# Block transposes on VectorE for K and the outputs in the second pass of a hybrid decoder layer

## The chip, the cores and the metric

The kernel runs on one core of a Trainium2 chip. The core has five engines with a queue each: TensorE (PE, matrix products and its own transposes), VectorE (DVE), ScalarE (ACT), GpSimd (POOL), and SyncE (SP, which here issues most of the DMAs). Each works through its own list of instructions in order and waits at semaphores for the others. The metric is the device time of one execution in microseconds (us), lower is better. The kernel before takes 1733.4 us, the median of three runs that lie between 1732.51 and 1734.95 us.

## The reference, cut to what matters

One layer over 2048 tokens of width 1024: a normed input `h`, one large input projection, a pooling branch A, a gated linear recurrence B (HGRN2, eight heads of 128), a gated merge, an output projection and a residual. The change touches branch B only:

```python
f = lb + (1.0 - lb) * jax.nn.sigmoid(zf)          # forget gate
logf = jnp.log(jnp.maximum(f, 1e-30))
k = 1.0 - f
q = jax.nn.silu(hq.astype(jnp.float32)).reshape(shp)
v = hi.astype(jnp.float32).reshape(shp)
o = hgrn2(q, k, v, logf)                          # S_t = diag(f_t) S_{t-1} + k_t v_t^T, o_t = S_t^T q_t
o = rms_norm(o, hgrn_norm_g[l]).astype(x.dtype).reshape(b, s, HGRN_WIDTH)
branch_b = (o * jax.nn.silu(hg)) @ w_hgrn_o[l]
```

In chunks, the recurrence needs three things of K: the scores of K against Q inside a chunk (channels must lie on the partitions), the update of the state `k * decay to the end of the chunk` against V (tokens must lie on the partitions), and, for the output, the scores against V plus Q against the state. The output comes out with tokens on the partitions, is normed there, and is needed with channels on the partitions for the next projection. So K and the output each have to be transposed once.

## The kernel before, in words

The tokens are worked in two passes of 1024 (p = 0, 1), each in two halves t = 0, 1 of T = 512 columns, that is four chunks of 128. All data is fp32; large products are formed from a high and a low part (three matmuls per weight tile, `three`, L355), and a Strassen-like scheme (`quad`, L625) makes the two column halves of two projections from seven products B11, T1, T2, B21, T3, B22, T4 of twelve matmuls each. Several products add into one PSUM bank one after another, and in between the bank is read. So T4 adds into bank `a` behind T3, and VectorE must first have read that bank for the sum at L651 (`c22fq<-pafq,c22fq` in the `fq` quad).

For each head h, three quads follow one another: `fq` (forget gate and query), `m` (the merge gates) and `gp` (pooling value or gate, and the output gate); in the last head `gp` comes before `m`. After each product but the first, and once after each quad, `htick` steps every active generator to its next `yield`. That is 21 ticks for each head.

`hgrn` (L677) is such a generator, one for each head and half. Its ticks, counted from the end of the head's `fq`:

- ticks 1 to 3 make F, K, the products TT of the decays and the first operands.
- tick 5, 9 and 14 run `scores` (32 small matmuls of K against X on PE into the bank `psa`), copy the masked results to PT on VectorE (`put`, L720) and multiply K and Q by decays (`kup` and `qup`, L710 to L716).
- tick 19 runs the last sixteen small score matmuls; then `kup(32)` and `kup(64)` (L812, L813) bring K to the end of the chunk.
- tick 21: four PE transposes bring K into the PSUM tile `pk` (L819), and ScalarE copies it to SBUF as `KS` (L821).
- tick 23: `pd` = KS against V (L826), and a chain of four VectorE instructions to carry the state `SC` (L831).
- tick 26: `po`, the output (L839, L840), its sums of squares on ScalarE, and the norm's factor on GpSimd.
- tick 28: ScalarE scales `po` to `on` in SBUF (L854).
- tick 30: four PE transposes bring `on` into the PSUM tile `pot` (L859), VectorE multiplies by the norm's weight and the gate (L861), and SP stores the result (`Gd`, L1026).

Ticks 22 and later fall into the next head, whose own generators run beside them: tick 30 of one head is tick 9 of the next. A pair of generators (t = 0, 1) is stepped in each tick, so transposes come in groups of eight. `pv_got` (L866, even heads) and `pg_got` (L889, odd heads) put the pooling branch's VectorE work into the `gp` quad, that is into ticks 9 to 15; the chain of `W` additions in `pv_got` has one step in head 0, two in head 2, three in head 4 and four in head 6.

The order on PE in the second pass is fixed by hand: with `line["on"]` every matmul and transpose is tied behind the one before it (L345 to L353). The order on the other engines is set by a scheduler that goes by a cost model and the order of the program: an instruction is moved ahead where it is ready and the engine would be idle. SBUF tiles come from one pool of NU = 76 slots (`utile`), PSUM tiles `pk`, `pd`, `po` and `pot` from a pool of two (`px`). Weights for the quads are loaded by SP four tiles ahead (LOOK = 4).

Of the kernel before, what the change touches and what calls it, by code (L numbers as in the profile page):

```python
# [8 lines left out]
F32 = mybir.dt.float32  # L9
# [9 lines left out]
P = 128  # L19
SEQ = 2048  # L20
D = 1024
T = 512
NT = T // P
# [3 lines left out]
NH = 8  # L27
# [8 lines left out]
GAP = 5  # L36
# [36 lines left out]
def tile_block(ctx: ExitStack, tc: tile.TileContext, x, w_ada, b_ada, g_post, w_in, pool_w, w_pool_o, w_hgrn_o,  # L73
               w_out, ident_d, mask_d, icnt_d, w_pv_t, x_t, w_quad, w_po, rows_d, out):
    nc = tc.nc
    V, A, G, PE, SP = nc.vector, nc.scalar, nc.gpsimd, nc.tensor, nc.sync
# [14 lines left out]
    px = ctx.enter_context(tc.tile_pool(name="px", bufs=2, space=bass.MemoryType.PSUM))  # L91

    def utile(name, dt=F32):
        return up.tile([P, T], dt, tag="u", name=name)
# [4 lines left out]
    def after(ins):  # L99
        return tc.issue_after(ins.ins) if ins is not None else nullcontext()  # L100
# [245 lines left out]
    def mm(o, l, r, start, stop):  # L346
        with after(line["it"] if line["on"] else None):
            line["it"] = PE.matmul(o, lhsT=l, rhs=r, start=start, stop=stop, skip_group_check=True)  # L348
        return line["it"]

    def turn(o, i):
        with after(line["it"] if line["on"] else None):
            line["it"] = PE.transpose(o, i, ident)  # L353

    def three(ps, w, rhs, start, stop):  # L355

        hi, lo = w
        n = len(rhs)
        for k in range(n):
            wh, wl = hi[:, k * P:(k + 1) * P], lo[:, k * P:(k + 1) * P]  # L360
            rh, rl = rhs[k]
            mm(ps, wh, rh, start and k == 0, False)
            mm(ps, wh, rl, False, False)
            mm(ps, wl, rh, False, stop and k == n - 1)
# [126 lines left out]
    def v2(ap, n):  # L491
        return ap.rearrange("p (a b) -> p a b", b=n)

    def bc(ap, n):
        return ap.unsqueeze(2).broadcast_to([P, ap.shape[1], n])

    def tt(o, a, b, op=MUL, e=None):
        return (e or V).tensor_tensor(o, a, b, op=op)  # L498
# [126 lines left out]
    def quad(name, cx, got, tick):  # L625
# [3 lines left out]
        def prod(ps, nm, start):  # L629
            three(ps, take(), [mv[nm, i] for i in range(4)], start, True)  # L630
# [45 lines left out]

    def hgrn(p, h, t, cx):  # L677
        n = f"{p}_{h}_{t}"
        F, Q = cx["F"].pop((h, t)), cx["Q"].pop((h, t))
        A.activation(F, F, AF.Identity, bias=lb[:, h:h + 1], scale=oml[:, h:h + 1])  # L680
        V.tensor_scalar(F, F, 1e-30, None, op0=MAX)  # L681
# [2 lines left out]
        K = utile("K" + n)  # L684
# [5 lines left out]
        o = 0  # L690
        for hh in (1, 2, 4, 8, 16, 32, 64):
            w = T // (2 * hh)
            a = v2(Tb[hh], 2)
# [10 lines left out]
        def te(hh, i):  # L704
            return v2(Tb[hh], 2)[:, :, i]

        def vv(cc):
            return vh[:, t * NT + cc, :]

        def kup(hh):  # L710
            a = v2(K, 2 * hh)[:, :, 0:hh]
            tt(a, a, bc(te(hh, 1), hh))

        def qup(hh):
            a = v2(Q, 2 * hh)[:, :, hh:2 * hh]
            tt(a, a, bc(te(hh, 0), hh))  # L716
# [3 lines left out]
        def put(dst, src):  # L720

            w = src.shape[2]
            if len(dst.shape) == 3:
                m = mask[:, moff[0]:moff[0] + 4 * w].rearrange("p (a b) -> p a b", b=w)
                moff[0] += 4 * w
                shp = [P, NT, 4, w]
                V.copy_predicated(dst.rearrange("p (c a) b -> p c a b", c=NT), m.unsqueeze(1).broadcast_to(shp),  # L727
                                  src.unsqueeze(2).broadcast_to(shp))
                return
            a, b = dst.shape[2:]  # L730
            m = mask[:, moff[0]:moff[0] + NB * w].rearrange("p (c q a b) -> p c q a b", c=NT, q=4, b=b)
            moff[0] += NB * w
            V.copy_predicated(dst.rearrange("p (c q) a b -> p c q a b", c=NT), m,  # L733
                              src.rearrange("p c (a b) -> p c a b", b=b).unsqueeze(2)
                              .broadcast_to([P, NT, 4, a, b]))

        def blk(ap, b, hh):

            r = ap.rearrange("p (b a w) -> p b a w", b=b, w=2 * hh)[:, :, :, hh:2 * hh]
            return r[:, :, 0, :] if T // b == 2 * hh else r  # L740
# [12 lines left out]
        def scores(X):  # L753
            for i in range(NB):
                r0 = (i % 4) * 32
                mm(s48[r0:r0 + 32, i // 4, 0:48], K[:, i * 32:(i + 1) * 32], X[:, i, :], True, True)
# [25 lines left out]
        for hh in (2, 8):  # L782
            scores(X)
            put(blk(ptf, NB, hh), s48[:, :, 0:16])
            put(blk(ptf, NB, 2 * hh), s48[:, :, 16:32])
            put(blk(ptf, NB, 2 * hh), s48[:, :, 32:48])
            kup(hh)
            kup(2 * hh)
            if hh == 2:
                X = build(8, NB, 16)  # L790
            else:
                X = qp.tile([P, T], F32, tag="qr", name=f"X32_{n}")
                x32 = X[:, 0:T // 2].rearrange("p (b w) -> p b w", w=32)
                A.copy(x32, blk(Q, NB // 2, 32))
                qup(32)
                x64 = X[:, T // 2:T].rearrange("p (b w) -> p b w", w=64)
                tq = Tb[32].rearrange("p (a b) -> p a b", b=4)
                q64 = blk(Q, NT, 64)
                tt(x64, q64, bc(tq[:, :, 1], 64))
            for _ in range(GAP):  # L800
                yield
        s64 = s48
        for cc in range(NT):
            o = cc * P
# [4 lines left out]
        A.copy(pt[0:64, :, 64:128], s64[0:64, :, 32:96])  # L809
        A.copy(pt[0:32, :, 32:64], s64[0:32, :, 0:32])  # L810
        A.copy(pt[64:96, :, 96:128], s64[64:96, :, 0:32])
        kup(32)  # L812
        kup(64)  # L813
        tt(q64, x64, bc(tq[:, :, 0], 64))
        yield
        yield
        pk = px.tile([P, T], F32, tag="px", name="pk" + n)
        for cc in range(NT):
            turn(pk[:, cc * P:(cc + 1) * P], K[:, cc * P:(cc + 1) * P])  # L819
        KS = utile("KS" + n)  # L820
        A.copy(KS, pk)  # L821
        yield
        yield
        pd = px.tile([P, NT, P], F32, tag="px", name="pd" + n)
        for cc in range(NT):
            mm(pd[:, cc, :], KS[:, cc * P:(cc + 1) * P], vv(cc), True, True)  # L826
        SC = utile("SC" + n)
# [3 lines left out]
            V.scalar_tensor_tensor(nxt, sts[-1], Tb[128][:, cc:cc + 1], pd[:, cc, :], op0=MUL, op1=ADD)  # L831
            sts.append(nxt)
        carry[h] = sts[NT]
        yield
        yield
        yield
        po = px.tile([P, NT, P], F32, tag="px", name="po" + n)
        for cc in range(NT):
            mm(po[:, cc, :], pt[:, cc, :], vv(cc), True, False)  # L839
# [12 lines left out]
        on = utile("on" + n)  # L852
        for cc in range(NT):
            A.activation(on[:, cc * P:(cc + 1) * P], po[:, cc, :], AF.Copy, scale=ss[:, cc:cc + 1])  # L854
        yield
        yield
        pot = px.tile([P, T], F32, tag="px", name="pot" + n)
        for cc in range(NT):
            turn(pot[:, cc * P:(cc + 1) * P], on[:, cc * P:(cc + 1) * P])  # L859
        og = cx["G"].pop((h, t))  # L860
        V.scalar_tensor_tensor(og, pot, col("ng"), og, op0=MUL, op1=MUL)  # L861
        two_out("G", p, h, t, og, cx, h == NH - 1)
# [507 lines left out]
    for p in range(NPASS):  # L1370
# [3 lines left out]
        if p == 0:  # L1374
# [14 lines left out]
            late = [lambda k=k: h_in(0, 1, k, cxs[0]) for k in range(KT)]  # L1389
# [48 lines left out]
        for h in range(NH):  # L1438
            if 0 < h < NH - 1:
                v_head(p, h + 1, cx)  # L1440
            n = f"{p}_{h}"
# [80 lines left out]
        late = []  # L1522
# [75 lines left out]
```

## Time and profile before

| | |
|---|---|
| median of three runs | 1733.4 us |
| the profiled execution, its own time | 1732.42 us |
| span in its profile | 1730.6 us |
| PE busy | 1706.8 us (99%) |
| VectorE busy | 1223.3 us (71%) |
| ScalarE busy | 853.2 us (49%) |
| granted TensorE clock | 1.0 |
| transposes on PE (`pk` and `pot`, both passes) | 256 |

The page of the profile gives busy time of each engine, the chain of waits that ended last, and groups of instructions. A view by stretches of time gives the busy time of every engine in each stretch; the timeline lists single instructions with start, duration, engine, line, and what they write and read ("sq" is Q, "c22fq" and "c12fq" are results of the quad that become Q and F). `x8` means eight instructions merged in one row, and the duration is then from the first start to the last end. Matmuls are pipelined, so the duration of one is longer than the distance from its start to the next one's. The heads of the second pass run from about 981 to 1535 us of the span, 69.2 us each.

### The profile page before, as it was taken

Reading aid. Unit: us, or ns where it says so; the run is one execution under the profiler, and the core shown is the slowest. Engines: PE = TensorE matmul, PEld = TensorE weight load, DVE = VectorE, ACT = ScalarE, POOL = GpSimd, SP = SyncE. Lnnn points to the kernel's source line nnn. Section 1 sums busy time; section 2 is a strip of 40 time slices with the busy share of each in tenths; the row PEclk is TensorE's granted clock in tenths of the full one; section 3 lists DMA queues with packets and bytes.
Section 4 is the critical chain, followed back from the end, with each engine's and each line's share of the span. In section 5 each row is a group of like instructions: output and inputs, shape, how many; then the busy total and the mean of one; then the engine's idle time right before and its main releaser. Section 6 shows DMA issues by size and latency. Waiting matters only on the chain.

```text
span 1730.6 us, 31715 instructions
## 1 busy us (share of the span) xinstructions
PE 1706.8 (99%) x11805; PEld 1405.1 (81%) x11805; DVE 1223.3 (71%) x2546; ACT 853.2 (49%) x1951; POOL 96.5 (6%) x151
## 2 busy tenths in 40 slices
PE   7999999999999999999999999999999999999998
PEld 4788888888888887878888888888888888888886
DVE  4668888897988889788787254455455545776666
ACT  5746656566565665342755334344343343434243
POOL 1100000000000000100030000000000000000002
PEclk9999999999999999999999999999999999999999
DMA  9759888788789788976795765665655655565657
GB/s 331 259 185 323 287 303 287 286 300 314 268 293 329 262 289 286 350 252 223 267 313 179 249 208 179 205 202 176 214 193 173 220 180 194 184 226 168 212 197 265
DMA packets 191262, 425.33 MB, mean 246 GB/s; under 512 B 19282, under 2 KB 44546, under 8 KB 191108
## 3 DMA queue, kind: packets, MB, share of 16 engines
q1 hardware_dynamic: 181748, 406.46, 69.2%
q10 hardware_dynamic: 9360, 16.85, 2.6%
q8 instruction: 93, 1.52, 0.4%
q14 instruction: 61, 0.50, 0.1%
HBM read 267.51 MB, written 155.71 MB: 245 GB/s over the span
## 4 chain that ended last, share of the span: by engine, by line
PE 91%; DVE 4%; DMA 2%; ACT 2%; issue 1%; SPq 0%; POOL 0%; DVEq 0%; ACTq 0%; POOLq 0%
PE pafq L348 10%; PE pagp L348 10%; PE pam L348 9%; PE psA L348 5%; PE pegp L348 5%; PE pefq L348 5%; PE pem L348 5%; PE psV L348 4%; PE raB L348 4%; PE psa L348 4%; PE ray L348 3%; PE pbfq L348 3%; PE po L348 2%; PE pbgp L348 2%; PE pbm L348 2%; PE raV L348 2%
## 5 line engine op out<-in xcount | busy, mean ns | idle before, releaser
L193 DVE TENSOR_TENSOR whl<-wr,whl 128x512 fp32r<-128x512 f32 x160 | 109.4, 689 | 38.1 <-ACT whl L192 31.2
L192 ACT CAST whl<-wr 128x512 fp32r<-128x512 f32 x160 | 99.5, 625 | 69.6 <-issue 18.0
L348 PE MATMUL pam<-hT,whl 128*128 128x512 f32 x384 | 128.2, 394 | 0.6 <-ACT c12m L634 0.5
L348 PE MATMUL pagp<-hT,whl 128*128 128x512 f32 x384 | 128.1, 394 | 0.4 <-ACT c12gp L634 0.4
L348 PE MATMUL pafq<-hT,whl 128*128 128x512 f32 x384 | 126.3, 390 | 0.0
L192 ACT CAST whl<-wri 128x512 fp32r<-128x512 f32 x76 | 47.1, 622 | 118.4 <-PE psA L348 31.5
L733 DVE COPY_PREDICATED PT<-mask,psa 128x256 f32<-128x256 uint8 x160 | 86.1, 547 | 11.9 <-PE psa L348 11.9
L348 PEld LDWEIGHTS pagp<-hT,whl 128*128 128x128 f32 x384 | 72.1, 188 | 16.3 <-ACT c12gp L634 0.5
L348 PEld LDWEIGHTS pam<-hT,whl 128*128 128x128 f32 x384 | 72.1, 188 | 15.8 <-ACT c12m L634 1.1
L348 PEld LDWEIGHTS pafq<-hT,whl 128*128 128x128 f32 x384 | 72.1, 188 | 15.2 <-ACT c12fq L634 0.2
L348 PE MATMUL psA<-Ph,whl 128*128 128x512 f32 x256 | 82.5, 395 | 0.6 <-ACT Ph L179 0.6
L348 PE MATMUL psV<-whl,hB 128*128 128x512 f32 x256 | 79.6, 394 | 1.2 <-ACT hB L1330 1.1
L498 DVE TENSOR_TENSOR K<-K,TT 128x256 f32<-128x256 f32 x192 | 80.4, 423 | 0.0
L348 PE MATMUL pagp<-lT,whl 128*128 128x512 f32 x192 | 74.9, 390 | 0.0
L348 PE MATMUL pam<-lT,whl 128*128 128x512 f32 x192 | 74.8, 390 | 0.0
L348 PE MATMUL pafq<-lT,whl 128*128 128x512 f32 x192 | 74.7, 389 | 0.0
L193 DVE TENSOR_TENSOR whl<-wri,whl 128x512 fp32r<-128x512 f32 x76 | 51.8, 686 | 23.8 <-ACT whl L192 23.0
L727 DVE COPY_PREDICATED PT<-mask,psa 128x256 f32<-128x256 uint8 (+1 forms) x96 | 52.0, 542 | 21.7 <-PE psa L348 21.7
L348 PEld LDWEIGHTS psa<-X,K 128*32 128x32 f32 x2816 | 48.6, 110 | 19.8 <-issue 17.5
L861 DVE SCALAR_TENSOR_TENSOR sgg<-pot,vec,sgg 128x512 f32<-128x512 f32 x32 | 23.1, 746 | 54.5 <-PE pot L353 54.5
L681 DVE TENSOR_SCALAR F<-F 128x512 f32<-128x512 f32 x16 | 6.8, 426 | 77.5 <-ACT F L680 77.4
L348 PEld LDWEIGHTS psV<-whl,hB 128*128 128x128 f32 x256 | 47.5, 188 | 14.0 <-ACT hB L1330 1.4
(568 smaller groups left out, 4786.7 us busy)
## 6 DMA issues: line engine op xcount, KB each, us to landing
wr<-in_w_quad_dram SPq DMA_DIRECT2D x88, 256.0 KB, 4.1
whl<-scr_y SPq DMA_DIRECT2D x36, 512.0 KB, 4.7
sm<-Sd SPq DMA_DIRECT2D x64, 256.0 KB, 5.3
whl<-scr_b SPq DMA_DIRECT2D x32, 512.0 KB, 4.0
scr_y<-rfy SPq DMA_DIRECT2D x40, 256.0 KB, 2.9
x<-in_x_dram SPq DMA_DIRECT2D x32, 256.0 KB, 4.8
wa<-in_w_ada_dram SPq DMA_DIRECT2D x32, 256.0 KB, 6.0
V<-Vd SPq DMA_DIRECT2D x16, 512.0 KB, 5.1
```

The lines of the kernel that those rows point to most:

```text
L192: A.copy(w[:, 0:T], raw)
L193: V.tensor_tensor(w[:, T:2 * T], raw, w[:, 0:T].bitcast(F32), op=SUB)
L348: line["it"] = PE.matmul(o, lhsT=l, rhs=r, start=start, stop=stop, skip_group_check=True)
L498: return (e or V).tensor_tensor(o, a, b, op=op)
L681: V.tensor_scalar(F, F, 1e-30, None, op0=MAX)
L727: V.copy_predicated(dst.rearrange("p (c a) b -> p c a b", c=NT), m.unsqueeze(1).broadcast_to(shp), src.unsqueeze(2).broadcast_to(shp))
L733: V.copy_predicated(dst.rearrange("p (c q) a b -> p c q a b", c=NT), m, src.rearrange("p c (a b) -> p c a b", b=b).unsqueeze(2) .broadcast ...
L861: V.scalar_tensor_tensor(og, pot, col("ng"), og, op0=MUL, op1=MUL)
```

## The change: block transposes on VectorE

In the second pass, heads 0 to 6 (`by_dve`), both transposes go from PE to VectorE. `V.transpose` turns 32x32 blocks; one instruction here takes 32 partitions and four chunks (32x128 elements) and writes them to another set of 32 partitions. Sixteen of them make one transpose of 128x512. `block_turn` issues four, for one group of 32 output partitions.

For K the scaled copy is made at tick 14, right behind the third scores, into a new tile KD (three VectorE multiplications in the place of the two `kup`s at tick 19), so that K itself stays as it is for the last scores. The turns into KS follow in ticks 15 to 18. `pk` and ScalarE's copy are gone. `pd` and the state's chain move from tick 23 to tick 21 in even heads (`late` = 2) and to tick 19 in odd heads; `po` stays at tick 26. The output is turned into an SBUF tile `ot` in ticks 31 to 34 (10 to 13 of the next head), and the multiplication at L861 and the store move from tick 30 to tick 34. In the first pass and in head 7 all stays as before.

```diff
+    def block_turn(dst, src, j):
+        d, s_ = (a.rearrange("p (c n) -> p c n", n=P) for a in (dst, src))
+        for i in range(4):
+            V.transpose(d[32 * j:32 * j + 32, :, 32 * i:32 * i + 32], s_[32 * i:32 * i + 32, :, 32 * j:32 * j + 32])
...
     def hgrn(p, h, t, cx):
         n = f"{p}_{h}_{t}"
+        by_dve, late = p > 0 and h < NH - 1, 2 * (h % 2 == 0)
...
                 tt(x64, q64, bc(tq[:, :, 1], 64))
-            for _ in range(GAP):
+                if by_dve:
+                    KD, KS = utile("KD" + n), utile("KS" + n)
+                    tt(v2(KD, 64)[:, :, 0:32], v2(K, 64)[:, :, 0:32], bc(te(32, 1), 32))
+                    for o in (0, 32):
+                        tt(v2(KD, P)[:, :, o:o + 32], v2((KD, K)[o // 32], P)[:, :, o:o + 32], bc(te(64, 1), 32))
+            for j in range(GAP):
+                if by_dve and hh == 8 and j:
+                    block_turn(KS, K if j == 4 else KD, j - 1)
                 yield
...
-        kup(32)
-        kup(64)
+        if not by_dve:
+            kup(32)
+            kup(64)
         tt(q64, x64, bc(tq[:, :, 0], 64))
-        yield
-        yield
-        pk = px.tile([P, T], F32, tag="px", name="pk" + n)
-        for cc in range(NT):
-            turn(pk[:, cc * P:(cc + 1) * P], K[:, cc * P:(cc + 1) * P])
-        KS = utile("KS" + n)
-        A.copy(KS, pk)
-        yield
-        yield
+        if by_dve:
+            for _ in range(late):
+                yield
+        else:
...
-        yield
-        yield
-        yield
+        for _ in range(7 - late if by_dve else 3):
+            yield
         po = px.tile([P, NT, P], F32, tag="px", name="po" + n)
...
-        yield
-        yield
-        pot = px.tile([P, T], F32, tag="px", name="pot" + n)
-        for cc in range(NT):
-            turn(pot[:, cc * P:(cc + 1) * P], on[:, cc * P:(cc + 1) * P])
+        if by_dve:
+            pot = utile("ot" + n)
+            yield
+            yield
+            for j in range(4):
+                yield
+                block_turn(pot, on, j)
+        else:
...
         og = cx["G"].pop((h, t))
         V.scalar_tensor_tensor(og, pot, col("ng"), og, op0=MUL, op1=MUL)
```

More of the change, by code (lines that the diff above doesn't have):

```diff
@@ L811, in hgrn @@
         A.copy(pt[64:96, :, 96:128], s64[64:96, :, 0:32])
-        kup(32)
-        kup(64)
+        if not by_dve:
+            kup(32)
+            kup(64)
         tt(q64, x64, bc(tq[:, :, 0], 64))
-        yield
-        yield
-        pk = px.tile([P, T], F32, tag="px", name="pk" + n)
-        for cc in range(NT):
-            turn(pk[:, cc * P:(cc + 1) * P], K[:, cc * P:(cc + 1) * P])
-        KS = utile("KS" + n)
-        A.copy(KS, pk)
-        yield
-        yield
+        if by_dve:
[4 more added lines that the diff above has]
+            yield
+            pk = px.tile([P, T], F32, tag="px", name="pk" + n)
+            for cc in range(NT):
+                turn(pk[:, cc * P:(cc + 1) * P], K[:, cc * P:(cc + 1) * P])
+            KS = utile("KS" + n)
+            A.copy(KS, pk)
+            yield
+            yield
         pd = px.tile([P, NT, P], F32, tag="px", name="pd" + n)
@@ L833, in hgrn @@
         carry[h] = sts[NT]
-        yield
-        yield
-        yield
+        for _ in range(7 - late if by_dve else 3):
+            yield
         po = px.tile([P, NT, P], F32, tag="px", name="po" + n)
@@ L854, in hgrn @@
             A.activation(on[:, cc * P:(cc + 1) * P], po[:, cc, :], AF.Copy, scale=ss[:, cc:cc + 1])
-        yield
-        yield
-        pot = px.tile([P, T], F32, tag="px", name="pot" + n)
-        for cc in range(NT):
-            turn(pot[:, cc * P:(cc + 1) * P], on[:, cc * P:(cc + 1) * P])
+        if by_dve:
+            pot = utile("ot" + n)
+            yield
+            yield
+            for j in range(4):
+                yield
+                block_turn(pot, on, j)
+        else:
+            yield
+            yield
+            pot = px.tile([P, T], F32, tag="px", name="pot" + n)
+            for cc in range(NT):
+                turn(pot[:, cc * P:(cc + 1) * P], on[:, cc * P:(cc + 1) * P])
         og = cx["G"].pop((h, t))
```

## The prediction

> **What bounds the kernel now.** I read the page, then the view by stretches for single heads of the second pass, then the timelines of PE and VectorE there.
>
> ```profile
> span 1730.6 us, 31715 instructions
> PE 1706.8 (99%) x11805; PEld 1405.1 (81%) x11805; DVE 1223.3 (71%) x2546; ACT 853.2 (49%) x1951; POOL 96.5 (6%) x151
> PE 91%; DVE 4%; DMA 2%; ACT 2%; issue 1%; SPq 0%; POOL 0%; DVEq 0%; ACTq 0%; POOLq 0%
> ...
> 1257.80:1327.00 69.20, 69.20 (x574) 57.96 (x573) 39.03 (x96) 28.54 (x75) 2.40 (x4) 1.00 0.59 191
> 1327.00:1396.20 69.20, 69.20 (x574) 57.95 (x573) 36.55 (x92) 27.76 (x71) 2.40 (x4) 1.00 0.62 198
> ```
>
> The last two rows are an even head (4) and an odd one (5): the stretch, its length, then busy PE, weight loads, VectorE, ScalarE, GpSimd, the clock, the DMA share. PE is never idle, at a granted clock of 1.00. VectorE works 36.55 to 39.03 of 69.2 us. So PE work taken out here is time won, as long as no new wait of PE on VectorE appears.
>
> **What PE gives up.** How long a matmul is listed says nothing of its price, since they overlap; I go by starts. First `pot` with the scores behind it and a place where the same scores follow a product directly; then `pk`, and a plain change of product.
>
> ```profile
> 1292.76 0.40 PE L348 MATMUL pegp<-hT,whl 128*128 128x512 f32 x1
> 1293.00 1.03 PE L353 MATMUL pot<-ident,on 128*128 128x128 f32 x8
> 1293.96 0.89 PE L348 MATMUL psa<-X,K 128*32 128x48 f32 x64
> ...
> 1308.31 0.39 PE L348 MATMUL pagp<-hT,whl 128*128 128x512 f32 x1
> 1308.63 0.89 PE L348 MATMUL psa<-X,K 128*32 128x48 f32 x64
> ...
> 1327.41 0.39 PE L348 MATMUL pefq<-hB,whl 128*128 128x512 f32 x1
> 1327.64 0.39 PE L348 MATMUL pafq<-hT,whl 128*128 128x512 f32 x1
> 1327.86 0.39 PE L348 MATMUL pafq<-lT,whl 128*128 128x512 f32 x1
> ...
> 1399.32 0.39 PE L348 MATMUL pafq<-hT,whl 128*128 128x512 f32 x1
> 1399.55 1.03 PE L353 MATMUL pk<-ident,K 128*128 128x128 f32 x8
> 1400.34 0.48 PE L348 MATMUL pam<-hB,whl 128*128 128x512 f32 x1
> 1400.66 0.40 PE L348 MATMUL pam<-lB,whl 128*128 128x512 f32 x1
> ```
>
> Eight `pot` transposes cost (1293.96 - 1292.76) - (1308.63 - 1308.31) = 0.88 us; eight `pk` cost (1400.66 - 1399.32) - (1327.86 - 1327.41) = 0.89 us. A head has one group of each. Seven heads: 7 x 1.77 = **12.4 us** off PE. That is the most the change can bring; the listed 272 ns each would say 30 us, and would be wrong. ScalarE's copy of `pk` goes too, 14 x 0.59 us, but ScalarE works 28 of 69 us in these heads and nothing waits on this copy except `pd`: I count it as nothing. `pd`, `po` and the scores keep their number.
>
> ```profile
> L821 ACT COPY KS<-pk 128x512 f32<-128x512 f32 x16 | 8.6, 593 | 0.0
> ```
>
> **What VectorE takes on.** A pair of generators issues 2 x 16 turns for K and 2 x 16 for the outputs: 64 a head, 448 in all, each 128 elements long on 32 partitions. No VectorE transpose is in the trace. The nearest rows are instructions of 128 elements:
>
> ```profile
> L831 DVE SCALAR_TENSOR_TENSOR SC<-SC,TT,pd 128x128 f32<-128x128 f32 x56 | 19.4, 346 | 1.7
> L498 DVE TENSOR_TENSOR TT<-TT 128x128 f32<-128x128 f32 x16 | 4.5, 284 | 0.0
> ...
> 1340.28 0.28 DVE L498 TENSOR_TENSOR TT<-TT 128x128 f32<-128x128 f32 x1
> 1340.48 0.34 DVE L831 SCALAR_TENSOR_TENSOR SC<-SC,TT,pd 128x128 f32<-128x128 f32 x1
> ```
>
> The lower end is 0.20 us, the distance from that TENSOR_TENSOR's start to the next start: neighbours overlap by 0.08 us. The upper end is 0.346 us, the dearest instruction of this length, with no overlap. I take the whole 0.284 us of the SBUF-to-SBUF row, without overlap, since each turn reads and writes other partitions than the one before it, which no instruction in these rows does. The Trainium skill bears on this choice and speaks against the change. Its page "VectorE: DVE Perf Modes", section "Two Vector instructions with no wait between them", says that an instruction whose input or output starts in another group of 32 partitions than the last one's is held until every earlier one has finished; the overlap rows above are all of instructions that start at partition 0, so no run here shows it. By that rule 0.284 is right and 0.20 is not.
>
> Call the price c. 64c is 18 us a head, and VectorE has 30 free on the mean. The mean doesn't decide: it must be done **by two dates**. The turns of outputs can begin when `on` is there (four of each half); the K turns end before `pd` in odd heads (tick 19), and in even heads before `c22fq` (L651), which stands behind them in program order and must read its bank before T4.
>
> ```profile
> 1288.24 0.36 ACT L854 ACTIVATE on<-po,ss 128x128 f32<-128x128 f32 x1
> 1288.75 1.92 ACT L854 ACTIVATE on<-po,ss 128x128 f32<-128x128 f32 x7
> ...
> 1323.38 0.69 DVE L498 TENSOR_TENSOR c22fq<-pafq,c22fq 128x512 f32<-128x512 f32 x1 [0.81 <-PE pafq L348]
> 1324.10 0.42 DVE L498 TENSOR_TENSOR sq<-X,TT 128x256 f32<-128x256 f32 x1
> 1324.77 0.69 DVE L498 TENSOR_TENSOR sq<-c22fq,sq 128x512 f32<-128x512 f32 x1
> ...
> 1326.05 0.42 DVE L498 TENSOR_TENSOR sq<-X,TT 128x256 f32<-128x256 f32 x1
> 1326.38 0.42 DVE L498 TENSOR_TENSOR K<-K,TT 128x256 f32<-128x256 f32 x1
> ...
> 1392.56 0.69 DVE L498 TENSOR_TENSOR c22fq<-pafq,c22fq 128x512 f32<-128x512 f32 x1 [0.75 <-PE pafq L348]
> 1393.28 0.43 DVE L498 TENSOR_TENSOR sq<-X,TT 128x256 f32<-128x256 f32 x1
> ...
> 1405.91 1.95 PE L348 MATMUL pd<-V,KS 128*128 128x128 f32 x16
> ...
> 1151.40:1189.20 37.80, 37.80 (x347) 31.02 (x347) 20.58 (x45) 11.45 (x28) 0.00 (x0) 1.00 0.60 198
> 1289.70:1327.60 37.90, 37.90 (x348) 31.11 (x347) 21.80 (x47) 11.61 (x28) 0.00 (x0) 1.00 0.62 199
> 1428.10:1465.90 37.80, 37.80 (x348) 31.01 (x347) 23.00 (x49) 11.51 (x28) 0.00 (x0) 1.00 0.60 197
> ...
> 1082.20:1117.20 35.00, 35.00 (x335) 28.69 (x334) 16.71 (x36) 9.26 (x19) 0.00 (x0) 1.00 0.66 215
> ...
> 1359.00:1394.00 35.00, 35.00 (x336) 28.70 (x334) 16.77 (x37) 9.26 (x19) 0.00 (x0) 1.00 0.68 217
> ```
>
> The first three stretches, heads 2, 4 and 6, run from the first half's `on` (the fourth of eight ends near 1289.7) to the start of T4 (1327.64). Head 4: VectorE is busy 21.80 us, of which 2.7 lie behind `c22fq` (1324.10 to 1326.80), so 19.1 us are due before it. KD adds per half one multiplication of 256 elements (0.33 us from start to start, 1326.05 to 1326.38) and two of 128 (0.20): 1.5 us for both. The two `kup`s that go, 4 x 0.33 us, lay behind `c22fq` and free nothing in time. The stretch loses `pot`'s 0.9 us. Room: 37.9 - 0.9 - 19.1 - 1.5 = 16.4 us for 64 turns, c up to 0.256. Likewise head 2: 37.8 - 0.9 - 17.9 - 1.5 = 17.5, c up to 0.274; head 6 (one more `W` in each half) 15.1, c up to 0.236. In the odd heads 1, 3 and 5 (the first and the last of three like stretches are shown) the date is `pd`, at 1394.0. Busy 16.7, less the 1.4 from `c22fq` on (1392.56), which isn't due before `pd`: 15.3. The second half's `pd` needs its KS about 0.85 us later than the first's (half of the 1.7 us over which the sixteen matmuls start). Room: 35.0 - 0.9 + 0.85 - 15.3 - 1.5 = 18.15, c up to 0.284. Head 0 has no outputs of a head before it in its stretch, so only half of the turns: no stall.
>
> At c = 0.284 PE is held up 64 x (0.010 + 0.028 + 0.048) = **5.5 us** in heads 2, 4 and 6, and nothing in the odd ones. Net 12.4 - 5.5 = 6.9 us. The profiled execution took 1732.42 us (its span plus 1.8), 1.0 below the median; from the median 1733.4 - 6.9 = **1727 us**.
>
> The ledger assumes that idle slots of VectorE are filled with turns that are ready; the trace shows the scheduler doing so (at 1324.10 tick 19's L814 runs ahead of the query's own multiplication of 1324.77, which is earlier in the program). The multiplication L861 only moves. The later output store stands on SP's queue ahead of weight loads; a load leaves about 9 us before its use and lands in 4.7:
>
> ```profile
> 1308.73 0.32 SPq L203 DMA_DIRECT2D whl<-scr_('fq', 5)_3_5551  x1
> 1317.74 0.39 PE L348 MATMUL pbfq<-hB,whl 128*128 128x512 f32 x1
> whl<-scr_y SPq DMA_DIRECT2D x36, 512.0 KB, 4.7
> ```
>
> So a store that is up to 4.3 us late costs nothing. `gp` is read back only after head 7. KS, KD and `ot` take SBUF slots in place of slots that `TT` and KS free earlier, because `pd` comes earlier; I count nothing.
>
> **The rivals.** (1) Turns overlap as other VectorE instructions do, c = 0.20 to 0.25: stalls are at most 0.9 us, in head 6, and PE keeps all 12.4 us: **1721 us**. For it: every pair of short instructions in the timeline overlaps. Against: none of them changes partitions.
>
> (2) The turn is dearer, and VectorE becomes the bound between `on` and T4 or `pd`. Past 0.284 the stalls sum to 64 x (6c - 1.617) us (1.617 is the sum of the six rooms); they eat the 12.4 us at c = 0.302, and from there on the kernel is **slower**. At the upper row, 0.346, they are 29.4 us: 1733.4 + 17.0 = **1750 us**. For it: the even heads are short of room already at 0.256. Against: transposes have one input and no PSUM operand, as the 346 ns row has.
>
> (3) c lies close to 0.30 and gain and stalls cancel: **1733 us**. The Trainium skill's same page, section "The three transpose paths", gives 311 ns for a VectorE transpose of 128x128 in bf16. By that figure and the hold, an estimate from the page, the sum would be 15.9 us of stalls and 1737 us.
>
> (4) A store of outputs waits on SP by more than the 4.3 us, because VectorE runs later than the scheduler assumed; the weight loads behind it come late. Three us past the slack in six heads would be 18 us against 12.4: **1739 us**. Against: the store's queue is free of this before.
>
> (5) The change doesn't act, because PE's transposes are hidden: excluded by the starts above, save 1 in 50.
>
> **How the numbers follow.** A measurement of this kernel can tell about 0.2%, 3.5 us, from no change; that is c from 0.293 to 0.311. Forecast (c from 0.25 to 0.293) 0.31; rival 1 0.21; rival 3 with 5 0.18; rival 2 0.25; rival 4 0.05. Faster 0.31 + 0.21 = 0.52, same 0.18, slower 0.30. The likeliest one's own range is 1721 to 1730. For 8 in 10 it must reach rival 1 (1721, less 2 for spread) and most of rival 2, to c = 0.34, where the stalls are 27.1 us: 1748.
>
> **What would show it.** PE's `pk` and `pot` groups fall from 128 to 72 each; the groups of VectorE show 448 turns at L358, and the distance between their starts is c. If I am right, PE idles a few us in heads 4 and 6 ahead of T4 (`pafq` waits for `c22fq`), less in 2, hardly in odd heads ahead of `pd`. No such wait: rival 1. Waits in all six: rival 2. Waits of PE on `whl`: rival 4. I am wrong if turns are cheap and PE still waits, or if `c22fq` is put ahead of the turns and `pd` alone is late.

## The result and the profile after

The changed kernel takes **1778.6 us** (median of four runs, 1778.2 to 1780.7) against 1733.6 of the kernel before on the same chip: a ratio of 1.0265, 95% interval 1.0253 to 1.0277. It is slower by 45 us, where 6.4 us faster was forecast. The profiled execution took 1780.71 us, with a span of 1778.9 us.

Rows of the page of the changed kernel: span, busy time of the engines, the chain that ended last by engine, and the three groups of turns (L358 is the transpose in `block_turn`).

```profile
span 1778.9 us, 31939 instructions
PE 1711.8 (96%) x11693; PEld 1401.5 (79%) x11693; DVE 1356.7 (76%) x3008; ACT 845.5 (48%) x1937; POOL 97.3 (5%) x151
...
PE 77%; DVE 16%; DMA 3%; issue 2%; ACT 1%; SPq 0%; POOL 0%; DVEq 0%; ACTq 0%; POOLq 0%
...
L358 DVE STREAM_TRANSPOSE ot<-on 32x128 f32<-32x128 f32 x224 | 67.8, 303 | 3.7
L358 DVE STREAM_TRANSPOSE KS<-KD 32x128 f32<-32x128 f32 x168 | 50.7, 302 | 2.2
L358 DVE STREAM_TRANSPOSE KS<-K 32x128 f32<-32x128 f32 x56 | 17.1, 305 | 0.8
```

The 448 turns are there, PE has 112 fewer instructions, and VectorE, which held 4% of the chain before, holds 16%. PE is at 96% instead of 99%. The view by stretches of the changed kernel: each of the first seven rows begins with the first product of a `fq` quad, those of heads 1 to 7, and the last row is the phase behind the heads (the stretch, its length, then busy PE, weight loads, VectorE, ScalarE, GpSimd, the granted clock, the DMA share, GB/s).

```profile
1036.20:1104.90 68.70, 67.68 (x564) 56.11 (x556) 51.10 (x150) 25.89 (x69) 2.42 (x4) 1.00 0.58 188
1104.90:1180.00 75.10, 69.55 (x564) 57.54 (x557) 55.12 (x156) 26.52 (x71) 2.40 (x4) 0.98 0.56 180
1180.00:1255.20 75.20, 69.34 (x565) 57.09 (x557) 57.11 (x164) 27.65 (x73) 2.40 (x4) 0.98 0.55 179
1255.20:1330.30 75.10, 69.50 (x562) 57.53 (x557) 55.22 (x155) 26.41 (x70) 2.40 (x4) 0.98 0.55 179
1330.30:1407.70 77.40, 70.22 (x562) 57.70 (x556) 58.29 (x167) 27.72 (x73) 2.40 (x4) 0.96 0.54 174
1407.70:1483.30 75.60, 70.00 (x566) 58.00 (x557) 55.24 (x155) 26.36 (x70) 2.40 (x4) 0.95 0.55 178
1483.30:1561.90 78.60, 70.11 (x563) 57.35 (x556) 65.23 (x178) 31.32 (x79) 2.40 (x4) 0.96 0.47 161
1561.90:1618.10 56.20, 53.96 (x328) 44.36 (x321) 44.06 (x84) 20.14 (x54) 2.40 (x4) 1.00 0.60 202
```

Before, each of the seven took 69.2 us at a clock of 1.00. Now the second to the seventh take 75 to 79 us, PE idles 5 to 9 us in each, and the granted clock is 0.95 to 0.98. VectorE, at 55 to 65 of these 75 to 79 us, is still not full. The view of PE's waits from 950 to 1630 us (what waited, for whom, us in all, times, the longest) says for what; the same view of the kernel before has no row.

```profile
PE pafq L348 <- DVE c22fq L503: 17.4, 3, 6.4
PE pd L348 <- DVE KS L358: 13.9, 3, 4.6
PE pagp L348 <- DVE c22gp L503: 5.9, 6, 1.0
PE psA L348 <- DVE Pl L179: 1.8, 2, 1.5
PE pam L348 <- DVE c22m L503: 1.2, 1, 1.2
PE pafq L348 <- ACT pbfq L644: 1.0, 1, 1.0
PE psa L348 <- DVE PT L733: 0.3, 1, 0.3
```

Three waits for `c22fq` are those of the even heads 2, 4, 6, three for `KS` those of the odd heads 1, 3, 5. These are the two dates of the prediction, with the even and the odd heads as it had them, but the odd ones, for which its sum had nothing, wait 4.6 us each. A third date, six waits for `c22gp`, it did not have. Together PE waits 41.5 us.

**Where the 48.3 us of span come from.** 12.4 off PE; 41.5 of waits; 3.5 us that the second pass's first head begins later (976.1 against 972.6 us), all in code that the change doesn't touch; it begins between 971.5 and 977.7 us in the runs below, so this is not put down to the change. From 1730.6 that makes 1763.2. Of the 15.7 us that are left, the clock takes up to 14.5: the lengths of the second to seventh row times what their clock lacks of 1.00 (three times 1.5, then 3.1, 3.8, 3.1). Some of that passes while PE waits anyway, so a few us are not placed one by one; a wait also costs a little more than the list says (between the starts around the longest wait of head 4, shown next, lie 6.55 us; without a wait it is 0.23, and the list has 6.16).

**How the clock falls**, around the longest wait of head 4. PE's timeline of the changed kernel (start, duration, what; in brackets the idle time before the row, and what ended it):

```profile
1348.25 0.39 PE L348 MATMUL pefq<-hB,whl 128*128 128x512 f32 x1
1354.80 0.79 PE L348 MATMUL pafq<-hT,whl 128*128 128x512 f32 x1 [6.16 <-DVE c22fq L503]
```

The stretches of the wait and of what follows it (columns as above):

```profile
1348.60:1352.90 4.30, 0.04 (x1) 0.00 (x0) 4.11 (x15) 0.00 (x0) 0.00 (x0) 1.00 0.36 122
1352.90:1359.70 6.80, 4.90 (x12) 3.84 (x13) 4.40 (x11) 2.08 (x3) 0.00 (x0) 0.50 0.00 0
```

For 6.8 us the clock is 0.50, from 1.9 us before the wait ends. PE works 4.9 of them, and half of that, 2.5 us, is lost on top of the wait.

The other two readings are from VectorE's timeline of the changed kernel in the same head:

```profile
1314.20 0.74 DVE L739 COPY_PREDICATED PT<-mask,psa 128x256 f32<-128x256 uint8 x1 [7.06 <-PE psa L348]
...
1317.97 5.01 DVE L358 STREAM_TRANSPOSE ot<-on 32x128 f32<-32x128 f32 x16
...
1343.91 7.55 DVE L358 STREAM_TRANSPOSE KS<-KD 32x128 f32<-32x128 f32 x24
```

and from ScalarE's, where `on` is made:

```profile
1308.74 0.36 ACT L871 ACTIVATE on<-po,ss 128x128 f32<-128x128 f32 x1
1309.25 1.92 ACT L871 ACTIVATE on<-po,ss 128x128 f32<-128x128 f32 x7
```

First, 24 turns back to back take 7.55 us, so starts are (7.55 - 0.30) / 23 = **0.315 us** apart, a little more than one turn's 0.303: no overlap at all. Second, `on` is complete at 1311.2, its first half at about 1310; VectorE is idle for the 7.06 us up to the puts at 1314.20, for which it waits on PE, and turns only afterwards, at 1317.97. An engine takes its list in order, and the turns are behind the puts in it. Room for 10 to 13 turns (3.0 to 4.1 us) passes unused in each of heads 1 to 6, where the outputs of heads 0 to 5 are turned.

### The profile page after: what moved, and what is told of

It reads as the page before. It is cut to its first block, busy times and chain, and to the rows that moved or that the text cites. A ratio compares the mean times of both kernels' runs of the same rounds, so it can differ in the third digit from the quotient of the medians.

```text
span 1778.9 us, 31939 instructions
## 1 busy us (share of the span) xinstructions
PE 1711.8 (96%) x11693; PEld 1401.5 (79%) x11693; DVE 1356.7 (76%) x3008; ACT 845.5 (48%) x1937; POOL 97.3 (5%) x151
## 4 chain that ended last, share of the span: by engine, by line
PE 77%; DVE 16%; DMA 3%; issue 2%; ACT 1%; SPq 0%; POOL 0%; DVEq 0%; ACTq 0%; POOLq 0%
PE pam L348 9%; PE pafq L348 7%; PE pagp L348 7%; PE psA L348 5%; PE pem L348 5%; PE psV L348 5%; PE pegp L348 4%; PE pefq L348 3%; DVE ot L358 3%; PE raB L348 3%; PE ray L348 3%; DVE KS L358 3%; PE psa L348 3%; PE po L348 3%; PE pbm L348 2%; PE pd L348 2%
## 5 line engine op out<-in xcount | busy, mean ns | idle before, releaser
L348 PE MATMUL pafq<-hT,whl 128*128 128x512 f32 x384 | 130.9, 402 | 18.3 <-DVE c22fq L503 17.4
L348 PEld LDWEIGHTS pam<-hT,whl 128*128 128x128 f32 x384 | 72.1, 188 | 17.4 <-DVE c22m L503 1.6
L358 DVE STREAM_TRANSPOSE ot<-on 32x128 f32<-32x128 f32 x224 | 67.8, 303 | 3.7
L503 DVE TENSOR_TENSOR K<-K,TT 128x256 f32<-128x256 f32 x164 | 69.4, 425 | 1.3 <-PE psa L348 1.3
L348 PE MATMUL psa<-X,K 128*32 128x48 f32 (+2 forms) x2816 | 60.6, 210 | 0.3 <-DVE PT L733 0.3
L865 POOL TENSOR_SCALAR ss<-ss 128x4 f32<-128x4 f32 x32 | 8.1, 254 | 926.0 <-ACT junk L864 892.3
```

The costliest lines, as they stand in the source:

```text
L358: V.transpose(d[32 * j:32 * j + 32, :, 32 * i:32 * i + 32], s_[32 * i:32 * i + 32, :, 32 * j:32 * j + 32])
L865: G.tensor_scalar(ss, ss, 1.0 / P, EPS, op0=MUL, op1=ADD)
```

## The experiments

The rest of the work was to tell apart the price of the turn, the number of turns, and the place where they stand. The kernel before had medians of 1732.4 to 1732.9 us beside these runs.

**One half of the change at a time.** *k_only*: K on VectorE as in the change, outputs transposed by PE as before.

```diff
-        if by_dve:
-            pot = utile("ot" + n)
...
+        if False:
+            pass
         else:
             yield
```

> K turned on VectorE, outputs on PE as before. Theory A (what PE waits for is turn time in front of two dates; a turn takes 0.315 us from start to start): in odd heads the K turns end about when pd needs them, in even heads about 0.4 to 0.8 us late for T4; no wait reaches 3 us and the clock stays at 1.00. 6.2 us come off PE, about 1.5 come back: about 1729 us (1727 to 1731). Theory B (the loss comes from pd's earlier tick, 19 or 21 where 23 was, and not from the number of turns): the waits of pafq on c22fq and of pd on KS stay as in the changed kernel, above 1755 us.

Measured: **1729.1 us** (1727.0 to 1731.6), ratio 0.9978 [0.9969, 0.9987]. Two heads in the view by stretches:

```profile
1100.90:1169.50 68.60, 68.60 (x573) 57.26 (x565) 45.98 (x125) 26.97 (x72) 2.40 (x4) 1.00 0.62 196
1169.50:1237.70 68.20, 68.20 (x568) 57.08 (x564) 47.20 (x132) 27.57 (x71) 2.40 (x4) 1.00 0.60 197
```

Its only row in the view of PE's waits:

```profile
PE pafq L348 <- DVE c22fq L503: 0.8, 2, 0.5
```

These heads are 0.8 us shorter on the mean than the 69.2 us of before; 32 turns a head fit at 0.315 us, as by theory A. The earlier step of `pd` does no harm by itself, so theory B falls.

*out_only*: outputs on VectorE, K as before (the conditions of the K part are set to `False`). *out_h5*: the same with outputs on VectorE only in heads 0 to 5:

```diff
-        if by_dve:
+        if by_dve and h < NH - 2:
             pot = utile("ot" + n)
```

> Outputs turned on VectorE, K on PE as before with pd at tick 23. Theory A: the 1.1 us waits of T4 in gp on c22gp stay in six heads (6 to 7 us), since the same output turns stand ahead of it; no wait on KS or c22fq, no half clock; 6.2 us come off PE, head 7 gives back some 2: 1733 to 1737 us. Theory B: nothing is moved forward, so all of PE's 6.2 us are kept: 1727 us.

> Outputs turned on VectorE in the first six heads only, K on TensorE as before. In the kernel with outputs on VectorE in seven heads (1741.6 us) the seventh head's turns stand among the last head's splits, and the last head and what follows it were about 5 us longer than before. Theory T (that tail is the seventh head's turns): the tail is as before, and the time is 1741.6 - 5 + 0.9 = 1737 us (1735 to 1739), still over before by the short waits on c22gp of some 1 us in each head. Theory U (the tail is put later by what the earlier heads push along): the time stays at 1740 to 1743 us.

Measured: out_only 1741.6 us, ratio 1.0044 [1.0029, 1.0059], slower than expected; out_h5 1737.1 us, 1.0029 [1.0019, 1.0039], as expected by theory T. The largest rows of PE's waits in out_only:

```profile
PE pagp L348 <- DVE c22gp L503: 5.9, 6, 1.0
PE psA L348 <- DVE Pl L179: 1.8, 2, 1.5
PE pam L348 <- DVE c22m L503: 1.2, 1, 1.2
```

In the same view of out_h5 the first of these rows is the only one with VectorE, word for word the same.

So the outputs alone already lose on the third date, 1.0 us in each of six heads, which more than eats the 0.88 that PE gives up: the heads of out_h5 take 69.5 to 69.8 us, against 69.2. Head 6's output turns run among the last head's splits and cost 1741.6 - 1737.1 + 0.9 = 5.4 us by themselves, for 0.9 us gained.

**The price of a turn.** *same_q* lets each turn stay in its own group of 32 partitions, and all K turns read K, where three of four had read KD; number, size and place of the turns are those of the change, and KS and the outputs hold other values.

```diff
-            V.transpose(d[32 * j:32 * j + 32, :, 32 * i:32 * i + 32], s_[32 * i:32 * i + 32, :, 32 * j:32 * j + 32])
+            V.transpose(d[32 * j:32 * j + 32, :, 32 * i:32 * i + 32], s_[32 * j:32 * j + 32, :, 32 * i:32 * i + 32])
...
-                    block_turn(KS, K if j == 4 else KD, j - 1)
+                    block_turn(KS, K, j - 1)
```

> Every turn reads and writes the same group of 32 partitions, in the place of crossing from one to another (K and the outputs hold other values than the reference's, the instructions and their order on VectorE are the same). Theory C (a turn waits for the one before it because it changes partitions): the distance of starts falls from 0.315 to about 0.22 to 0.24 us, the waits shrink by about 5 us a head, no half clock, 1725 to 1735 us. If the turn is simply that long: 0.315 stays and the time stays near 1778 us.

Measured: 1730.0 us (1728.4 to 1734.5), ratio 0.9975 [0.9964, 0.9985]. A row of VectorE's timeline:

```profile
1319.22 6.67 DVE L358 STREAM_TRANSPOSE KS<-K 32x128 f32<-32x128 f32 x32
```

Its largest waits of PE:

```profile
PE pafq L348 <- DVE c22fq L503: 4.2, 2, 2.9
PE pd L348 <- DVE KS L358: 0.5, 3, 0.2
```

32 turns in 6.67 us have starts (6.67 - 0.30) / 31 = 0.205 us apart, the overlap of the prediction's lower end. With that price nearly all waits go, although VectorE still idles ahead of the puts (7.06 us up to 1292.19): with turns this cheap, their place costs little. It is the partitions that keep a turn from overlapping the one before it. But which: that a turn crosses from one group to another, or that its groups differ from those of its predecessor? *after_pair* tells: the changed kernel, every turn crossing as before, but the turns of the two halves between the same two groups stand back to back.

```diff
-    def block_turn(dst, src, j):
-        d, s_ = (a.rearrange("p (c n) -> p c n", n=P) for a in (dst, src))
-        for i in range(4):
-            V.transpose(...)
+    half = {}
+
+    def block_turn(t, dst, src, j):
+        two = tuple(a.rearrange("p (c n) -> p c n", n=P) for a in (dst, src))
+        if t == 0:
+            half[j] = two
+            return
+        it = None
+        for i in range(4):
+            for d, s_ in (half[j], two):
+                with after(it):
+                    it = V.transpose(...)
```

> The changed kernel with the 32 turns of a kind in another order: the two halves' turns between the same two groups of partitions stand back to back, so that every second turn reads and writes the partition groups of the turn before it (and the gate's multiplication comes one step later). Theory Q (a turn is held until the one before has finished where its partitions differ from that one's): starts are 0.315 us apart ahead of every first of a pair and about 0.20 ahead of every second, some 0.26 on the mean; a head's 64 turns take 3.5 us less, the waits of pd (4.6) and c22fq (5.0 to 6.4) shrink by about that, most stretches of half clock go, and the time is 1743 us (1736 to 1752). Theory R (a turn across partition groups is slow by itself, whatever stands before it): starts stay 0.315 us apart and the time is 1774 to 1782 us.

Measured: 1756.7 us (1754.3 to 1761.9), ratio 1.0134 [1.0117, 1.0151]; past the upper end of theory Q, far from theory R. A row of VectorE's timeline:

```profile
1259.80 6.09 DVE L366 STREAM_TRANSPOSE KS<-KD 32x128 f32<-32x128 f32 x24
```

Its largest waits of PE:

```profile
PE pafq L348 <- DVE c22fq L511: 9.8, 3, 4.6
PE pd L348 <- DVE KS L366: 9.3, 3, 3.1
```

(6.09 - 0.30) / 23 = **0.252 us** on the mean: with 0.315 for the first of a pair, the second costs 0.19. A crossing turn overlaps as well as any other if its predecessor used the same groups. That is what the Trainium skill's page "VectorE: DVE Perf Modes", section "Two Vector instructions with no wait between them", says in its model of a held instruction; the two runs agree with it (0.315 held, 0.19 not).

The run tells something else too. At 0.252 us all rooms of the prediction but that of head 6 (0.236) are wide enough, and PE should have waited 64 x (0.252 - 0.236) = 1 us in all. It waited 19.1 at these two dates. The rooms were wrong, whatever the price.

**The place of the turns.** *k_late_o4*: K turns later (steps 19 to 22), `pd` at step 23 in every head, as before the change; output turns two steps later than in the change.

```diff
             for j in range(GAP):
-                if by_dve and hh == 8 and j:
-                    block_turn(KS, K if j == 4 else KD, j - 1)
                 yield
...
-            for _ in range(late):
+            for j in range(4):
+                block_turn(KS, K if j == 3 else KD, j)
                 yield
...
-        for _ in range(7 - late if by_dve else 3):
+        for _ in range(3):
```

> Same number of turns, later in the program: K's behind the last scores (ticks 19 to 22) with pd at tick 23 as before, the outputs' two ticks later (33 to 36). Theory A: c22gp and c22fq go ahead of turns, those waits vanish; pd waits up to 3 us in heads 4 and 6, where turns are short of room, none in odd heads: 12.4 us off PE, about 5 given back, 1726 us (1721 to 1734). If slots of the SBUF pool were the bound, tiles held longer would make it slower than the changed kernel, above 1780 us.

Measured: 1748.8 us (1748.2 to 1753.1), ratio 1.0096 [1.0076, 1.0115]; 1726 was expected. Its largest waits:

```profile
PE pd L348 <- DVE KS L358: 9.7, 6, 2.8
PE psa L348 <- DVE PT L733: 2.6, 2, 1.8
PE pafq L348 <- DVE c22fq L503: 2.5, 2, 1.7
```

Later places for both kinds of turns, with the later date of `pd`, cut the loss to about a third and don't end it: the idle stretch is still empty (7.05 us up to the puts at 1294.69 in this run).

*o_early* leaves all dates of the change and only calls the output turns right behind the norm, so that they stand ahead of the puts:

```diff
             pot = utile("ot" + n)
-            yield
-            yield
             for j in range(4):
-                yield
                 block_turn(pot, on, j)
+            for j in range(6):
+                yield
```

> The changed kernel with one edit: the four output block turns of a head stand right behind the norm (no steps between), so that they can run in VectorE's idle stretch ahead of the second half's first puts, and the store keeps its step. Theory G (the changed kernel lost about 4.2 us of VectorE time per head because its output turns stood behind the puts while the turns were ready and VectorE was idle): the waits of pd on KS (13.9 us in all, longest 4.6) and of pafq on c22fq (17.4, longest 6.4) lose up to 4.2 us each time and are 8 us or less in sum, the slow stretches of the clock mostly go, and the time is near 1778 - 23 - 10 = 1745 us (1735 to 1755). Theory H (the sum of VectorE's work between the dates decides, wherever it stands): the waits stay within 3 us of the changed kernel's sum and the time is 1772 to 1782 us. A wait of the second half's first products behind the puts may grow, by up to the length of the turns that start late: 32 x 0.315 = 10 us less the idle stretch.

Measured: 1750.9 us (1748.6 to 1755.0), ratio 1.0116 [1.0099, 1.0132]. All its waits of PE:

```profile
PE pagp L348 <- DVE c22gp L503: 15.6, 6, 2.7
PE pam L348 <- DVE c22m L503: 3.0, 1, 3.0
PE pafq L348 <- DVE c22fq L503: 1.7, 2, 1.2
```

The same number of turns at the same price: the waits for `KS` and `c22fq` fall from 31.3 to 1.7 us, and the time is in theory G's range. That refutes theory H and shows the unused stretch to be the main cause of those two; the waits for `c22gp`, now 2.5 to 2.7 us in place of 1.0, also give VectorE time, about 1.6 us a head. For 32 turns are 10 us, the stretch is 3 to 4, and `c22gp`, behind turns and puts, is late.

*mix* joins both edits: K late with `pd` at step 23, outputs only in heads 0 to 5, half of their turns right behind the norm and half five steps later.

> K is turned on VectorE in steps 19 to 22 and pd stands at step 23 in every one of the first seven heads; outputs are turned on VectorE in the first six heads only, half of them right behind the norm (into the idle stretch ahead of the puts), half five steps later. Theory G with the late date of pd: the stretches up to c22fq have room, no wait is over 1 us, TensorE gives up 7 x 0.89 + 6 x 0.88 = 11.5 us per group of K and outputs, and the time is 1733 - 11.5 = 1722 us (1720 to 1727), below the kernel with K alone on VectorE (1729). Theory H: the sum of VectorE's work is what it was with pd late (1749), less one head's output turns (10 us of VectorE, of which at most 5 on the path): 1743 to 1749 us.

Measured: 1750.8 us (1748.1 to 1754.7), ratio 1.0109 [1.0092, 1.0125]: a miss by theory G's own number, and close above theory H's 1743 to 1749. The only row of PE's waits:

```profile
PE pagp L348 <- DVE c22gp L503: 16.5, 6, 2.8
```

VectorE's timeline at the place:

```profile
1303.36 7.24 DVE L358 STREAM_TRANSPOSE ot<-on 32x128 f32<-32x128 f32 x23 [3.03 <-ACT on L870]
```

The stretch behind the first of these waits:

```profile
1102.90:1106.30 3.40, 3.40 (x10) 2.63 (x9) 2.38 (x4) 0.89 (x2) 0.00 (x0) 0.50 0.94 304
```

Not 16 but 23 turns stand ahead of the puts, though the second half was called five steps later: the scheduler had moved ahead what was ready. The steps of the program don't hold a turn back. So this run had not tried theory G's order, and the next one does.

*t2_5* is mix with the second half of the output turns tied behind the instruction that was late:

```diff
-        tt(s5, a, s5, op=ADD)
+        last["c22"] = tt(s5, a, s5, op=ADD)
...
             for j in range(2, 4):
-                block_turn(pot, on, j)
+                with after(last["c22"]):
+                    block_turn(pot, on, j)
                 yield
```

> The kernel mix with one edit: the second half of the output turns is tied behind the combination that frees the bank of pagp (c22gp), so that 8 of the 32 turns of a pair run in VectorE's idle stretch ahead of the puts and 24 run in the 7.3 us in which VectorE idles behind the next puts. Theory G (only where the turns stand decides, since VectorE has idle time enough): the wait on c22gp, 16.5 us in mix, is gone, the granted clock stays full through the heads, and the time is 1732.5 - 11.5 = 1721 us (1719 to 1725), 8 us below the kernel with K alone on VectorE. Theory H (the number of turns on VectorE decides): the waits move to another place (the late puts hold the last score products or c22fq) and the time stays over 1733 us.

Measured: **1725.2 us** (1723.8 to 1727.4), ratio 0.9959 [0.9945, 0.9973]. That is 25.6 us less than mix, by this edit alone. 16 turns now stand ahead of the puts and 16 behind `c22gp` (the expectation's 8 and 24 was a wrong count). PE's waits in the second pass are down to one of 0.2 us. One head in the view by stretches:

```profile
1168.70:1236.60 67.90, 67.77 (x563) 56.17 (x556) 57.69 (x164) 28.10 (x72) 2.81 (x4) 1.00 0.62 198
```

VectorE is as busy as in the changed kernel (57.7 us in this stretch, against 57.1 in the third row of the changed kernel), its turns are as dear, and every head takes 67.9 us at full clock. It has 416 of the 448 turns, all but those of head 6's outputs. Mix, with the same number of turns and the same date of `pd`, lost 18 us. So, with turns at this price, it is where they stood that lost most of the 45 us, and not their number; some 5 us go to head 6's outputs. The 0.5 us that a head takes more than hoped (69.2 - 1.77 = 67.4) are in `pd`, whose products start as their parts of KS come in.

*pair* is t2_5 with the order by pairs of after_pair.

> The kernel t2_5 (every turn placed into VectorE's idle stretches) with the same order by pairs. Theory Q: the K turns end some 2 us earlier, so that the 0.5 us by which a head's sixteen pd products were spread out go; seven heads give 3 us, and the time is 1722 us (1719 to 1725). Theory R: the time is that of t2_5, 1725 us (1723 to 1728).

Measured: **1720.2 us** (1719.5 to 1720.6), ratio 0.9927 [0.9913, 0.9942], the fastest of all. Its page, busy time and the chain by engine:

```profile
PE 1694.9 (99%) x11701; PEld 1392.7 (81%) x11701; DVE 1328.7 (77%) x2976; ACT 847.0 (49%) x1937; POOL 98.3 (6%) x151
...
PE 89%; DMA 4%; DVE 4%; ACT 1%; issue 1%; SPq 0%; POOL 0%; DVEq 0%; POOLq 0%; ACTq 0%
```

One head in the view by stretches:

```profile
1166.30:1233.70 67.40, 67.40 (x569) 56.19 (x557) 54.78 (x164) 28.10 (x72) 2.41 (x4) 1.00 0.62 200
```

PE is not idle for a moment in the heads. 69.2 - 67.4 = 1.8 us a head is the 1.77 that the prediction had read from the starts.

**The clock.** *ladder* puts further turns behind the K turns of k_late_o4, with the outputs on PE, so that PE waits for `KS`. They write the last block of KS once more.

```diff
+            for i in range((0, 2, 3, 4, 5, 6, 8)[h]):
+                V.transpose(KS.rearrange("p (c n) -> p c n", n=P)[96:128, :, 96:128], K.rearrange("p (c n) -> p c n", n=P)[96:128, :, 96:128])
```

> Outputs on TensorE, K on VectorE with pd at step 23, and behind the K turns 0, 4, 6, 8, 10, 12 and 16 further turns in heads 0 to 6 (they write what the turn before them wrote), so that TensorE waits for KS by steps of 0.6 us or more from head to head. Theory C (a wait of TensorE over some 2 to 2.6 us is followed by a granted clock of 0.5 for 3.4 or 6.8 us, and costs 1.7 or 3.4 us beside its own length): the clock is full after the heads with waits under 2 us and 0.5 after those over 2.6 us, wherever in the head the wait ends. Theory D (the half clock comes from something else that the changed kernel does, its turns or its products at that place): the clock is full in every head, or half after short waits too.

Measured, one profile: 1774.0 us. Its only row of PE's waits:

```profile
PE pd L348 <- DVE KS L832: 28.7, 6, 6.1
```

PE's timeline at the first of them:

```profile
1133.35 2.90 PE L348 MATMUL pd<-V,KS 128*128 128x128 f32 x12 [3.73 <-DVE KS L832]
```

The stretch around it:

```profile
1132.40:1139.20 6.80, 5.85 (x22) 5.40 (x23) 5.58 (x19) 1.81 (x5) 0.00 (x0) 0.50 0.01 2
```

The first step was too large: head 0 has no wait, and the next is already 3.7 us long, so the part of theory C on short waits was not tested here (the other runs have such waits, see the last section). The half clock appears in all six heads with a wait, 6.8 us at a time, with the outputs back on PE. t2_5 and pair have the turns of K and of outputs, no wait over 0.2 us, and a clock of 1.00 in their heads. So the half clock goes with the wait and not with the turns, and theory D falls. 28.7 us of waits went with 1774.0 - 1729.1 = 45 us more than k_only takes.

## Why the prediction was wrong, point by point

- **What PE gives up**, 1.77 us a head: right. pair has 1.8, k_only 0.8 for `pk` alone (0.89 forecast).
- **The price of a turn**, "the whole 0.284 us of the SBUF-to-SBUF row, without overlap": right that nothing overlaps and why, too low in size. It is 0.315. By the prediction's own formula that is 64 x (6 x 0.315 - 1.617) = 17.5 us of stalls instead of 5.5 (11.5 in the even heads, 6.0 in the odd ones): 1739 us, still 40 short. Measured were 17.4 in the even heads and 13.9 in the odd ones. The 311 ns that the prediction gave from the Trainium skill's page "VectorE: DVE Perf Modes", section "The three transpose paths", were nearer than the row that I took.
- **"The ledger assumes that idle slots of VectorE are filled with turns that are ready; the trace shows the scheduler doing so."** This is the step that failed. One place where an instruction ran ahead was taken for a rule. The changed kernel left 3 to 4 us of a head's stretch empty while the turns were ready (the row at 1314.20), o_early filled them and lost the waits for `KS` and `c22fq`, and after_pair waited 19.1 us where the rooms allowed 1. A room counted as length minus busy time holds only if nothing in front of the new work waits. The trace of before had the warning in it. In head 4's stretch, which begins at 1289.70, VectorE idles up to 1293.64, where it waits for PE, and the puts come behind that:

```profile
1293.64 1.41 DVE L861 SCALAR_TENSOR_TENSOR sgg<-pot,vec,sgg 128x512 f32<-128x512 f32 x2 [6.99 <-PE pot L353]
1294.96 0.72 DVE L733 COPY_PREDICATED PT<-mask,psa 128x256 f32<-128x256 uint8 x1
```

These 3.9 us were in the room of 16.4 us that the prediction gave to head 4.
- **"By two dates"**: there were three. `c22gp`, which frees a bank of the `gp` quad, stands behind the output turns and was 1.0 us late in six heads; with the outputs alone it was enough to turn the gain into a loss.
- **A granted clock of 1.00**: the prediction took over the clock of before and gave a stall its own length. Stalls of 4.6 to 6.4 us were followed by 3.4 or 6.8 us at half clock. This step was missing altogether.
- **"Head 0 has no outputs ... only half of the turns: no stall"**: right; but its counterpart at the end, head 6's outputs in head 7, was not costed, and takes 5.4 us (out_only less out_h5).
- **What was counted as nothing**: ScalarE's copy, the later store, the SBUF slots. Nothing in the changed kernel's waits names them, and pair, which has all three, has no wait in the heads. Rival 4 falls: no product of the heads waits for `whl` in the changed kernel. Rival 5 falls with pair.
- **The rivals**: rival 2 had the side, the mechanism and the heads (all six wait), at a price of 0.346 and 1750 us. The turn was cheaper than that and the loss larger, for the two reasons above.
- **"I am wrong if turns are cheap and PE still waits"**: that is after_pair.

## What to carry to other kernels

Room on an engine is not its idle time: work fits only where it stands in the engine's order between what is late and what is due, so count from the list, and look at every wait on another engine that lies between. If a unit that sets the time must wait at all, price the wait with what follows it, here half a clock for 3.4 or 6.8 us. Where work is to fill a gap, tie it behind the instruction that it must not delay, and put instructions that use the same partition groups next to each other.

## What the runs showed of the hardware

- A 32x128 transpose of 4-byte values on VectorE takes 0.303 us; starts are 0.315 us apart if its groups of 32 partitions differ from its predecessor's, about 0.19 to 0.205 if not, even where source and destination groups differ from each other.
- How long PE must wait before the clock falls, over all traces (their starts and last 30 us left out): a stretch at 0.50 began within the wait or up to 2.5 us behind its end for none of 28 waits of 0.9 to 1.3 us, 5 of 12 of 1.5 to 2.1 us, 14 of 19 of 2.5 to 3.0 us, and all 16 of 3.1 to 6.4 us. It lasted 3.4 or 6.8 us.
- In each run these stretches begin on one grid: those in the changed kernel's heads begin at 1124.24, 1202.74, 1274.42, 1352.93, 1424.61 and 1506.53 us, which are 23, 21, 23, 21 and 24 times 3.413 us apart. So the same wait can go either way by when it falls: of three waits of 2.52 us in o_early, one was followed by half a clock and two were not.
- The Trainium skill's page "TensorE: Matmul & The Clock Gate", section "Part 1: The HAM clock gate", has the clock halved after an idle window of about 3.4 us whose phase runs freely. The lengths of 3.4 and 6.8 us and the grid agree with it; that waits of 1.5 to 3.0 us were often enough does not, if the whole window must be idle. How much of it must be was not settled.
